# Mixer of a hybrid decoder step: loaded bias tables, HGRN2 factors on VectorE, row sums in two short-format passes, a fifth block-product pair

## The chip, the core and the metric

The kernel runs on one core of one Trainium2 chip. The metric is the device time of one execution in microseconds (us); the time given for a kernel is the median of its runs. The engines are named as in the profile: PE (TensorE, matrix products; PEld is its weight load), DVE (VectorE), ACT (ScalarE), POOL (GpSimd) and SP (SyncE, which here only issues DMAs). SBUF is the memory on the chip, in 128 partitions; PSUM, in eight banks, takes the matmul results, and POOL cannot read it.

## The reference, cut to what matters

One layer works on 544 tokens: 512 of a prompt and 8 x 4 of a sample group. The model width is 1024; the mixer has 8 attention heads of 64 and 4 HGRN2 heads of 128.

```
h = RMSNorm(x); z = h @ W_in        # 28 tiles of 128 columns: q, k, v (4 each), HGRN2 q, f, i, gate (4 each)
# dilated attention: three patterns (128,1), (512,4), (2048,16), penalty -m_h * distance, combined by
#   their softmax denominators; then every head RMS-normalised
# HGRN2: f = lb + (1-lb)*sigmoid(z_f); S_t = diag(f_t) S_{t-1} + (1-f_t) outer i_t;
#   o_t = S_t^T silu(q_t) / sqrt(128); per-head RMSNorm, times silu(gate)
x += [attn ; hgrn] @ W_out
x += CrossAttn(RMSNorm(x); 256 memory rows, K/V made from RMSNorm(mem)) @ W_co
x += W_down( silu(conv3(RMSNorm(x) W_gate)) * (RMSNorm(x) W_up) )
y = RMSNorm(x)
```

The three patterns are one softmax over all keys up to the query, with a bias: key distance d gets -m_h * d + ln(number of patterns that hold d). For the prompt this bias, for a block of 128 queries, is one table of 128 x 512 per head; the blocks use its right-hand parts.

## The kernel before, in words

Activations lie transposed (channels on partitions, 544 tokens along the free dimension). Most products are done in a short format: a matrix is split into a high part (a copy to float32r, on ACT) and a low part (the difference, on DVE), and a product is three passes, high x high, high x low and low x high. A plain tile of `z` is 8 x 3 products for tokens 0 to 255 and as many for 256 to 543 (`CUTS`, `passes`, `half`, `dense`). Other products, the row sums among them, are done in full float32; the profile shows such a matmul as two records.

**Block products.** `MixPair` makes two tiles of `z` together. It cuts the two weight tiles into four half-depth blocks and the tokens into two halves of 272, and computes the result from seven block products of 12 short-format matmuls in place of eight, at the price of sums of weight blocks (`S1` to `S4`), their own high and low parts, and sums of results. The token-side blocks are made once (`blocks_in`). `MIX_ORDER` lists the tiles in order; names that stand together are such a pair (four pairs in the kernel before), the others are plain tiles (`proj_in`). `ready` starts what can begin with a tile: `prompt_attention` for a v tile, `hgrn` when a head has its four tiles.

**Attention.** `prompt_attention(p, ...)` handles two heads. It makes their two bias tables on DVE, each with one `scalar_tensor_tensor` of the constants `dist` and `lnc`. Then, for three groups of query blocks: scores on PE, bias and row maximum on DVE, exp on ACT, normalisation on DVE, transposes and the value products on PE. Last it squares the output, sums it over each head's 64 rows by a matmul with a 0/1 matrix (`rsqrt_rows` with `blk64`) and scales.

**HGRN2.** `hgrn(h, ...)` works in seven levels of doubling width w (1 to 64; `level_ops`). At each level, DVE multiplies k by G and q by f, POOL multiplies half of G by the last f of the neighbouring half, and DVE multiplies half of f by the other's last. The f product writes what the POOL operation reads, so it waits for it. PE takes the products of the level (`level_products`). `hgrn_norm` ends a head with squares, a row sum (`rsqrt_rows` with `ones`, once per cut) and the gate.

**Norms.** `NextNorm` collects the squares of a new x, tile by tile, in `acc` (`SumSq`): ACT squares, POOL adds. `rows(c)` then takes the row sum of a cut with `rsqrt_rows`. The first norm of the kernel (`r_mix`), the memory's and the final one do their own full-format sums.

**Decode attention and order.** The sample group's attention over its cache (`decode_attention`) streams some 30 MB from memory as a side work of the mixer, in small products. What sets the order is `Tape`: it records all instructions as steps with dependencies and estimated lengths, and then plans one order per engine queue. PE's main steps (the tiles) keep their order; side steps on PE are put in as bursts, and the other queues take, among the steps that are ready, the one due first. `LEAD` is how far ahead of its due time a step may be taken, `MARGIN` the time to spare before a main step, `BURST` and `PATIENCE` say when a burst begins; `SLACK` gives steps their due time and is stored with each step as it is recorded. `run` plans `ROUNDS` = 4 orders, the due times of the second to fourth taken from the starts of the one before, and emits the one with the earliest planned end of PE. Tiles of kind "a" share `NA` = 59 buffers, weights 3 raw and 2 high and low ones, and PSUM banks fall into three kinds ("dense", "aux", "dec"). All compute instructions go through one wrapper line, L642, so the profile tells them apart by the names of their tiles.

Of the kernel before, what the change touches and what calls it, by code (L numbers as in the profile page):

```python
# [42 lines left out]
FW = 564  # L43
NA = 59

# [16 lines left out]
MIX_RAW = 3  # L62
MIX_ORDER = ('i0', 'q0', 'q1', 'q2 q3', 'k0 k1', 'k2 k3', 'f1 Q1', 'v0', 'g1', 'i1', 'v1', 'f2', 'Q2', 'g2', 'i2', 'v2', 'f3', 'Q3', 'g3', 'i3', 'v3')
WO_ORDER = (4, 5, 6, 0, 1, 7, 2, 3)
# [17 lines left out]
for _n, _c in (("ident", 128), ("ones", 128), ("blk64", 128), ("dist", 512), ("lnc", 512), ("dbias", NR + 2 * NS),  # L82
               ("mask_a", 96), ("mask_b", 96), ("mask_s", 96), ("batch", 4), ("h8", 8), ("h4", 4), ("sel8", 16),
               ("sel4", 16), ("sel32", 32), ("own", 2)):
    _span(CST_COLS, _n, _c)
# [10 lines left out]
def _log_counts(d):  # L96
    c = _counts(d)
    return np.where(c > 0, np.log(np.maximum(c, 1)), NEG)


def _constants():
# [11 lines left out]
    dist = 384 + p[:, None] - np.arange(512)[None, :]  # L113
    put("dist", dist.astype(np.float32))
    put("lnc", _log_counts(dist))
    slopes = 2.0 ** -(np.arange(NH) + 1.0)
    h = (p % 32) // TS
    t = p % TS
# [133 lines left out]
class Tape:  # L252
# [6 lines left out]

    ROUNDS = 4  # L260
    BURST, PATIENCE, SLACK, LEAD, MARGIN = 1.0, 4.0, 12.0, 15.0, 4.0
# [151 lines left out]
    def run(self):  # L413

        scale = sum(s.length for s in self.steps if s.engine == "PE") / sum(s.length for s in self.mains)
        t = 0.0
        for s in self.mains:
            s.est = t
            t += s.length * scale
        best = None  # L420
        for _ in range(self.ROUNDS):
            done = self.order()
            end = max(s.end for s in done if s.engine == "PE")
            if best is None or end < best[0]:
                best = end, done
            for s in self.mains:
                s.est = s.start
        for s in best[1]:
            for call in s.calls:
                call()  # L430
        self.live = False
        return done
# [214 lines left out]
def tile_decoder_step(ctx: ExitStack, tc: tile.TileContext, xT, memT, kwT, vw, s0, conv_in, mkT, mv, vecs, cst,  # L647
# [42 lines left out]
    nc.scalar.dma_start(vec, vecs)  # L690
    mid = CST_COLS["dist"][0]
    cs = tape.tile(one, [128, mid], F32, name="cs")
    cs2 = tape.tile(strm, [128, NCST - mid], F32, name="cs2")
    eps = tape.tile(one, [128, 1], F32, name="eps")
# [170 lines left out]
    def split_plain(src, name):  # L865
# [3 lines left out]
        return hi, lo  # L869

    def rsqrt_rows(acc, c0, c1, mat, width, r, name):

        for n0, m in ((c0, c1 - c0),) if c1 - c0 <= 512 else CUTS:
            ps = PX(f"psr_{name}_{n0}")
            nc.tensor.matmul(ps[:, :m], mat, acc[:, n0:n0 + m], start=True, stop=True)
            nc.scalar.activation(r[:, n0:n0 + m], ps[:, :m], AF.Ln, bias=eps, scale=1.0 / width)
            nc.scalar.activation(r[:, n0:n0 + m], r[:, n0:n0 + m], AF.Exp, scale=-0.5)
# [54 lines left out]
    with tape.as_written():  # L932
# [12 lines left out]
        for i in range(3):  # L945
            ws.load(i)
        nc.sync.dma_start(cs2, cst[:, mid:])
        for _ in range(AHEAD - 1):
# [34 lines left out]


    lbt = tape.tile(strm, [128, 4, 4], F32, name="lbt")
    l0 = vec[:, VEC_COLS["lb0"][0]:VEC_COLS["lb0"][1]]
# [271 lines left out]
    def decode_finish(out):  # L1258
# [18 lines left out]
        nc.scalar.activation(sq[:, :128], flat, AF.Square)  # L1277
        rsqrt_rows(sq, 0, 128, C("blk64"), 64, r, "attS")
        nc.vector.tensor_tensor(flat, flat, r[:, :128], op=ALU.mult)
# [9 lines left out]
    def prompt_attention(p, q, k, v):  # L1289
# [4 lines left out]
        for hh in range(2):  # L1294
            nc.vector.scalar_tensor_tensor(bias[hh][:, :512], C("dist"), -(2.0 ** -(2 * p + hh + 1)), C("lnc"),
                                           op0=ALU.mult, op1=ALU.add)
        S, P, T, PT, dens = {}, {}, {}, {}, {}
# [87 lines left out]
        nc.scalar.activation(sq[:, :SEQ], po, AF.Square)  # L1385
        rsqrt_rows(sq, 0, SEQ, C("blk64"), 64, r, f"att{p}")
        nc.vector.tensor_tensor(att[:, :SEQ], att[:, :SEQ], r[:, :SEQ], op=ALU.mult)
# [6 lines left out]
    def hgrn(h, f, q, gt, v):  # L1394
# [25 lines left out]
        def level_ops(w):  # L1420
# [12 lines left out]
            last = half(f, 1)[:, :, w - 1:w].to_broadcast([128, nb, w])  # L1433
            nc.gpsimd.tensor_tensor(half(G, 0), half(G, 0), last, op=ALU.mult)
            last = half(f, 0)[:, :, w - 1:w].to_broadcast([128, nb, w])
# [139 lines left out]
    def hgrn_norm(h, o, gt):  # L1575
# [3 lines left out]
        r = A(f"hr{h}")  # L1579
        for n0, n in CUTS:  # L1580
            rsqrt_rows(sq, n0, n0 + n, C("ones"), 128, r, f"hg{h}")
        nc.vector.tensor_tensor(o[:, :N], o[:, :N], r[:, :N], op=ALU.mult)
# [133 lines left out]
    class NextNorm:  # L1716


        def __init__(self, gain, name):
            self.gain, self.name, self.ssq, self.r = gain, name, SumSq(name, nc.gpsimd), A(f"r_{name}")  # L1720
            self.hl = [None] * KT
# [8 lines left out]
        def rows(self, c):  # L1730
            n0, n = CUTS[c]
            rsqrt_rows(self.ssq.acc, n0, n0 + n, C("ones"), D, self.r, self.name)

# [685 lines left out]
```

## Time and profile before

| what | value |
|---|---|
| median of 3 runs | 826.87 us (825.66 to 828.18) |
| profiled execution | 827.21 us, of which the span of instructions 825.4 us |
| mean granted TensorE clock | 0.996 |
| DMA | 132.32 MB, mean 160 GB/s |
| table loads on ACT | 11, 1283 ns each |

In the profile a group of instructions has its engine, operation, the names written and read (buffer numbers left out), shapes, count, busy time and mean; "idle before" is how long the engine sat without work ahead of such an instruction, with what ended that. Matmuls overlap, so the length of one record is longer than the step from one start to the next; the same holds, by some 0.07 us, for DVE. The mixer ends at about 316 us, where the `ps_wo` products begin; cross attention follows to 442, the first plain FFN tiles to 488, the FFN's block products and down products to 792, and the last down products and the final norm to the end.

### The profile page before, as it was taken

Reading aid. Unit: us, or ns where it says so; the run is one execution under the profiler, and the core shown is the slowest. Engines: PE = TensorE matmul, PEld = TensorE weight load, DVE = VectorE, ACT = ScalarE, POOL = GpSimd, SP = SyncE. Lnnn points to the kernel's source line nnn. Section 1 sums busy time; section 2 is a strip of 40 time slices with the busy share of each in tenths; the row PEclk is TensorE's granted clock in tenths of the full one; section 3 lists DMA queues with packets and bytes.
Section 4 is the critical chain, followed back from the end, with each engine's and each line's share of the span. In section 5 each row is a group of like instructions: output and inputs, shape, how many; then the busy total and the mean of one; then the engine's idle time right before and its main releaser. Section 6 shows DMA issues by size and latency. Waiting matters only on the chain.

```text
span 825.4 us, 18881 instructions
## 1 busy us (share of the span) xinstructions
PE 813.9 (99%) x7551; PEld 762.4 (92%) x7551; DVE 617.2 (75%) x1316; ACT 419.0 (51%) x835; POOL 148.0 (18%) x239
## 2 busy tenths in 40 slices
PE   9999999999999999999999999999999999999996
PEld 9999877887888889999889998999999999999995
DVE  6987889866879887564576998976777677767754
ACT  7643455434458345444545456554554455545533
POOL 0030211110210200222323131121112111211013
PEclk9999999999999999999999999999999999999999
DMA  9439999557823444260721347456456645653503
GB/s 343 156 121 297 352 287 304 166 170 226 289 81 110 158 145 153 59 218 31 256 86 53 103 103 203 130 131 176 118 140 181 139 116 145 163 149 83 164 1 109
DMA packets 90759, 132.32 MB, mean 160 GB/s; under 512 B 6064, under 2 KB 60080, under 8 KB 90544
## 3 DMA queue, kind: packets, MB, share of 16 engines
q1 hardware_dynamic: 84480, 120.69, 45.8%
q0 software_dynamic: 5184, 9.44, 7.2%
q8 instruction: 59, 0.97, 0.5%
q10 hardware_dynamic: 1008, 0.99, 0.4%
q14 instruction: 28, 0.23, 0.1%
HBM read 123.03 MB, written 8.07 MB: 159 GB/s over the span
## 4 chain that ended last, share of the span: by engine, by line
PE 91%; DVE 3%; ACT 2%; DMA 2%; issue 0%; SPq 0%; DVEq 0%; ACTq 0%
PE ps_d L642 13%; PE ps_au L642 6%; PE ps_ag L642 6%; PE ps_wo L642 6%; PE ps_cu L642 3%; PE ps_cg L642 3%; PE ps_z_v L642 3%; PE ps_co L642 3%; PE ps_g L642 3%; PE ps_cq L642 3%; PE ps_dz L642 3%; PE ps_u L642 3%; PE ps_z_g L642 2%; PE ps_z_i L642 2%; PE psdo L642 2%; PE psd L642 2%
## 5 line engine op out<-in xcount | busy, mean ns | idle before, releaser
L642 ACT CAST wh<-wr 128x1024 fp32r<-128x1024 f32 (+1 forms) x60 | 52.5, 889 | 73.6 <-issue 12.9
L642 DVE TENSOR_TENSOR wl<-wr,wh 128x1024 fp32r<-128x1024 f32 (+1 forms) x60 | 63.1, 1064 | 9.2 <-ACT wh L642 8.6
L642 DVE TENSOR_TENSOR xr<-xr,ps_d 128x256 f32<-128x256 f32 x80 | 34.5, 434 | 37.6 <-PE ps_d L642 37.5
L642 POOL COPY last<-ug 128x2 f32<-128x2 f32 (+1 forms) x44 | 14.7, 366 | 160.9 <-DVE ug L642 133.9
L642 DVE SCALAR_TENSOR_TENSOR cv<-ug,vec,cv 128x560 f32<-128x560 f32 x44 | 35.1, 798 | 8.1 <-ACT cv L642 7.8
L642 POOL TENSOR_TENSOR hG<-hG,z_f 128x256 f32<-128x256 f32 (+1 forms) x21 | 18.9, 899 | 118.9 <-DVE kq L642 63.5
L642 ACT ACTIVATE cv<-cv 128x560 f32<-128x560 f32 x22 | 14.8, 673 | 19.9 <-DVE cv L642 19.9
L642 ACT ACTIVATE cv<-ug,vec 128x560 f32<-128x560 f32 x22 | 18.8, 856 | 10.6 <-DVE ug L642 9.7
L617 POOL DMA_DIRECT2D S1u<-in_w_up x9 | 7.8, 862 | 89.4 <-DMA S1u<-in_w_up 45.3
L642 ACT ACTIVATE P<-P,mx 128x128 f32<-128x128 f32 (+3 forms) x32 | 17.7, 553 | 11.9 <-DVE mx L642 11.8
L642 POOL TENSOR_TENSOR acc_cx<-acc_cx,sq_cx 128x256 f32<-128x256 f32 (+1 forms) x14 | 11.4, 819 | 59.1 <-ACT sq_cx L642 59.0
L642 POOL COPY ug<-conv_state 128x16 f32<-128x16 f32 x22 | 18.4, 837 | 4.9 <-PE ps_u L642 2.8
L642 PE MATMUL ps_co<-coh,wh 128*128 128x256 f32 (+1 forms) x64 | 19.0, 297 | 0.0
L642 PE MATMUL ps_co<-coh,wl 128*128 128x256 f32 (+1 forms) x64 | 18.4, 288 | 0.0
L642 PE MATMUL ps_co<-col,wh 128*128 128x256 f32 (+1 forms) x64 | 18.4, 288 | 0.0
L642 POOL COPY qbd_win<-z_q 64x32 f32<-64x32 f32 x8 | 8.2, 1024 | 51.1 <-DVE z_q L642 50.9
L642 DVE TENSOR_TENSOR xr<-xr,ps_wo 128x256 f32<-128x256 f32 (+1 forms) x16 | 6.8, 435 | 13.9 <-PE ps_wo L642 13.8
L642 PE MATMUL psdo<-st,dpt 128*32 128x256 f32 x224 | 16.4, 386 | 0.0
L642 DVE TENSOR_TENSOR xr<-xr,ps_dz 128x288 f32<-128x288 f32 (+1 forms) x16 | 7.0, 436 | 12.3 <-PE ps_dz L642 12.3
L642 POOL TENSOR_TENSOR acc_ux<-acc_ux,sq_ux 128x256 f32<-128x256 f32 (+1 forms) x14 | 11.7, 834 | 20.9 <-ACT sq_ux L642 20.8
L642 PE MATMUL psd<-st,qbd_win 128*32 128x224 f32 x256 | 15.3, 358 | 0.0
L642 ACT ACT_TABLE_LOAD x11 | 14.1, 1283 | 2.3 <-issue 2.2
(3122 smaller groups left out, 3635.0 us busy)
## 6 DMA issues: line engine op xcount, KB each, us to landing
st<-in_kwT SPq DMA_DIRECT2D x32, 448.0 KB, 6.2
st<-in_vw SPq DMA_DIRECT2D x28, 512.0 KB, 5.7
wr<-in_w_in SPq DMA_DIRECT2D x17, 512.0 KB, 6.4
wd<-in_w_down SPq DMA_DIRECT2D x32, 256.0 KB, 2.8
wrg<-in_w_gate SPq DMA_DIRECT2D x9, 512.0 KB, 5.9
wru<-in_w_up SPq DMA_DIRECT2D x9, 512.0 KB, 4.6
st<-in_mkT SPq DMA_DIRECT2D x8, 512.0 KB, 6.8
wr<-in_w_out SPq DMA_DIRECT2D x8, 512.0 KB, 3.8
```

The costliest lines, as they stand in the source:

```text
L617: return tape.put(engine, lambda: call(*args, **kw), outs, ins, 0.1, 0.3, size)
L642: return tape.put(engine, lambda: call(*args, **kw), outs, ins, length, lag, size, port, words)
```

## The change

- **Bias tables.** The constants `dist` and `lnc` (512 columns each) are dropped, and eight finished tables (512 columns each) are laid behind the other constants in memory. `prompt_attention` loads its two with two DMAs of 256 KB on SP's queue instead of computing them. The early load of constants ends before these tables.
- **HGRN2 factors.** The product on G in `level_ops` goes from POOL to DVE.
- **Row sums.** `rsqrt_rows` splits the squares into a high part (a copy on ACT) and a low part (a subtraction on DVE), and sums both with a float32r copy of the 0/1 matrix, two short-format matmuls for one full-format one. The 0/1 matrices are copied once (`sum_operands`). `hgrn_norm` calls it once for all 544 columns; the matmuls inside are still cut in two.
- **Norm squares.** `NextNorm` lets DVE, and no longer POOL, add the squares. The final norm keeps POOL.
- **Fifth pair.** `v0` and `g1`, plain tiles before, become the pair `g1 v0`.
- **Order.** `run` plans 32 orders: the first with the constants as they are, the others with drawn values of `SLACK`, `LEAD`, `MARGIN`, `BURST` and `PATIENCE`. A draw that finds no order is left out. Due times are no longer taken from the order before. The random numbers have a fixed seed, so that the same order comes out each time.
- `NA` goes from 59 to 60 buffers.

```diff
-NA = 59
+NA = 60
-MIX_ORDER = (... 'f1 Q1', 'v0', 'g1', 'i1', 'v1', ...)
+MIX_ORDER = (... 'f1 Q1', 'g1 v0', 'i1', 'v1', ...)
...
-    put("dist", dist.astype(np.float32))
-    put("lnc", _log_counts(dist))
     slopes = 2.0 ** -(np.arange(NH) + 1.0)
+    put("bias", np.concatenate([(-s * dist + _log_counts(dist)).astype(np.float32) for s in slopes], 1))
...
-    ROUNDS = 4
+    DRAWS = 32
...
-        best = None
-        for _ in range(self.ROUNDS):
-            done = self.order()
+        best, draw = None, random.Random(0)
+        for i in range(self.DRAWS):
+            if i:
+                self.SLACK, self.LEAD, self.MARGIN = (draw.uniform(*r) for r in ((9.0, 16.0), (12.0, 19.0), (3.0, 6.0)))
+                self.BURST, self.PATIENCE = draw.uniform(0.6, 1.5), draw.uniform(2.5, 6.0)
+            try:
+                done = self.order()
+            except AssertionError:
+                continue
             end = max(s.end for s in done if s.engine == "PE")
             if best is None or end < best[0]:
                 best = end, done
-            for s in self.mains:
-                s.est = s.start
...
+    sums = {n: tape.tile(one, [128, 128], F32R, name=f"{n}_r") for n in ("ones", "blk64")}
+
+    def sum_operands():
+        for n, t in sums.items():
+            nc.scalar.copy(t, C(n))
+
     def rsqrt_rows(acc, c0, c1, mat, width, r, name):
+        hi, lo = R(f"sqh_{name}{c0}"), R(f"sql_{name}{c0}")
+        nc.scalar.copy(hi[:, c0:c1], acc[:, c0:c1])
+        nc.vector.tensor_tensor(lo[:, c0:c1], acc[:, c0:c1], hi[:, c0:c1].bitcast(F32), op=ALU.subtract)
         for n0, m in ((c0, c1 - c0),) if c1 - c0 <= 512 else CUTS:
             ps = PX(f"psr_{name}_{n0}")
-            nc.tensor.matmul(ps[:, :m], mat, acc[:, n0:n0 + m], start=True, stop=True)
+            for i, t in enumerate((hi, lo)):
+                nc.tensor.matmul(ps[:, :m], sums[mat], t[:, n0:n0 + m], start=i == 0, stop=i == 1)
...
-        nc.sync.dma_start(cs2, cst[:, mid:])
+        nc.sync.dma_start(cs2, cst[:, mid:end])
...
         for hh in range(2):
-            nc.vector.scalar_tensor_tensor(bias[hh][:, :512], C("dist"), -(2.0 ** -(2 * p + hh + 1)), C("lnc"),
-                                           op0=ALU.mult, op1=ALU.add)
+            nc.sync.dma_start(bias[hh][:, :512], cst[:, end + 512 * (2 * p + hh):end + 512 * (2 * p + hh) + 512])
...
-            nc.gpsimd.tensor_tensor(half(G, 0), half(G, 0), last, op=ALU.mult)
+            nc.vector.tensor_tensor(half(G, 0), half(G, 0), last, op=ALU.mult)
...
-        for n0, n in CUTS:
-            rsqrt_rows(sq, n0, n0 + n, C("ones"), 128, r, f"hg{h}")
+        rsqrt_rows(sq, 0, N, "ones", 128, r, f"hg{h}")
...
-            self.gain, self.name, self.ssq, self.r = gain, name, SumSq(name, nc.gpsimd), A(f"r_{name}")
+            self.gain, self.name, self.ssq, self.r = gain, name, SumSq(name), A(f"r_{name}")
```

More of the change, by code (lines that the diff above doesn't have):

```diff
@@ L1 @@
 import math
+import random
 from contextlib import ExitStack, contextmanager
@@ L62 @@
 MIX_RAW = 3
-MIX_ORDER = ('i0', 'q0', 'q1', 'q2 q3', 'k0 k1', 'k2 k3', 'f1 Q1', 'v0', 'g1', 'i1', 'v1', 'f2', 'Q2', 'g2', 'i2', 'v2', 'f3', 'Q3', 'g3', 'i3', 'v3')
+MIX_ORDER = ('i0', 'q0', 'q1', 'q2 q3', 'k0 k1', 'k2 k3', 'f1 Q1', 'g1 v0', 'i1', 'v1', 'f2', 'Q2', 'g2', 'i2', 'v2', 'f3', 'Q3', 'g3', 'i3', 'v3')
 WO_ORDER = (4, 5, 6, 0, 1, 7, 2, 3)
@@ L81 @@
     _span(VEC_COLS, _n, _c)
-for _n, _c in (("ident", 128), ("ones", 128), ("blk64", 128), ("dist", 512), ("lnc", 512), ("dbias", NR + 2 * NS),
+for _n, _c in (("ident", 128), ("ones", 128), ("blk64", 128), ("dbias", NR + 2 * NS),
                ("mask_a", 96), ("mask_b", 96), ("mask_s", 96), ("batch", 4), ("h8", 8), ("h4", 4), ("sel8", 16),
-               ("sel4", 16), ("sel32", 32), ("own", 2)):
+               ("sel4", 16), ("sel32", 32), ("own", 2), ("bias", 512 * NH)):
     _span(CST_COLS, _n, _c)
@@ L690, in tile_decoder_step @@
     nc.scalar.dma_start(vec, vecs)
-    mid = CST_COLS["dist"][0]
+    mid, end = CST_COLS["dbias"][0], CST_COLS["bias"][0]
     cs = tape.tile(one, [128, mid], F32, name="cs")
-    cs2 = tape.tile(strm, [128, NCST - mid], F32, name="cs2")
+    cs2 = tape.tile(strm, [128, end - mid], F32, name="cs2")
     eps = tape.tile(one, [128, 1], F32, name="eps")
@@ L982, in tile_decoder_step @@
             first_products(KT - 1)
+    sum_operands()
     lbt = tape.tile(strm, [128, 4, 4], F32, name="lbt")
@@ L1277, in decode_finish @@
         nc.scalar.activation(sq[:, :128], flat, AF.Square)
-        rsqrt_rows(sq, 0, 128, C("blk64"), 64, r, "attS")
+        rsqrt_rows(sq, 0, 128, "blk64", 64, r, "attS")
         nc.vector.tensor_tensor(flat, flat, r[:, :128], op=ALU.mult)
@@ L1385, in prompt_attention @@
         nc.scalar.activation(sq[:, :SEQ], po, AF.Square)
-        rsqrt_rows(sq, 0, SEQ, C("blk64"), 64, r, f"att{p}")
+        rsqrt_rows(sq, 0, SEQ, "blk64", 64, r, f"att{p}")
         nc.vector.tensor_tensor(att[:, :SEQ], att[:, :SEQ], r[:, :SEQ], op=ALU.mult)
@@ L1731, in rows @@
             n0, n = CUTS[c]
-            rsqrt_rows(self.ssq.acc, n0, n0 + n, C("ones"), D, self.r, self.name)
+            rsqrt_rows(self.ssq.acc, n0, n0 + n, "ones", D, self.r, self.name)
     cross_in = NextNorm("norm_cross", "cx")
```

## The prediction

> **What bounds the kernel now.** I read the page's head first, then the chain of waits, then the busy time by stage. From the page, the span, the busy shares and the chain's shares by engine:
>
> ```profile
> span 825.4 us, 18881 instructions
> PE 813.9 (99%) x7551; PEld 762.4 (92%) x7551; DVE 617.2 (75%) x1316; ACT 419.0 (51%) x835; POOL 148.0 (18%) x239
> PE 91%; DVE 3%; ACT 2%; DMA 2%; issue 0%; SPq 0%; DVEq 0%; ACTq 0%
> ```
>
> The matmul engine is busy nearly all the time and carries nine tenths of the chain. By stage (columns: stretch and length in us, busy time of PE, weight load, DVE, ACT, POOL, then granted clock, DMA share, GB/s); the last row is the whole mixer after its first products:
>
> ```profile
> 97.00:145.00 48.00, 48.00 (x710) 37.09 (x703) 43.20 (x143) 23.70 (x58) 9.24 (x11) 1.00 0.93 301
> 250.00:290.00 40.00, 40.00 (x498) 35.48 (x496) 36.64 (x101) 24.63 (x49) 6.60 (x7) 1.00 0.47 142
> 306.20:309.60 3.40, 3.40 (x10) 2.68 (x10) 1.88 (x4) 1.89 (x5) 0.00 (x0) 0.50 0.65 216
> 316.00:442.00 126.00, 126.00 (x1024) 119.32 (x1023) 75.19 (x145) 58.99 (x147) 32.73 (x41) 1.00 0.41 133
> 488.00:792.00 304.00, 302.50 (x2404) 301.70 (x2403) 232.26 (x432) 159.65 (x297) 48.22 (x106) 1.00 0.55 142
> 20.00:316.00 296.00, 294.36 (x3431) 251.69 (x3430) 245.61 (x618) 149.62 (x305) 43.57 (x52) 0.99 0.63 201
> ```
>
> The reader is to see three things. PE has no gaps to give back, so a gain must come from products taken away. DVE is second: 90% in 97 to 145 and 92% in 250 to 290, with 296.0 - 245.6 = 50.4 us idle over the mixer. And one short stretch, 306.2 to 309.6, ran at half the clock with PE busy throughout. The few real stalls show in the chain and in PE's timeline (start, length, what; the chain's rows come first):
>
> ```profile
> 90.69 1.28 ACT L642
> 92.43 1.77 PE ps_af1Q L642 x12
> 91.35 0.24 PE L642 MATMUL psd<-knew,qbd_win 128*32 128x32 f32 x8
> 502.68 0.39 PE L642 MATMUL ps_d<-h3h,wd_0h 128*128 128x256 f32 x1
> 503.45 0.38 PE L642 MATMUL ps_d<-h3l,wd_0h 128*128 128x256 f32 x1 [0.38 <-DVE h3l L642]
> 505.16 0.29 PE L642 MATMUL ps_du<-B21h,wlu 128*128 128x272 f32 x1
> 506.35 0.39 PE L642 MATMUL ps_au<-Uh,S2u4h 128*128 128x272 f32 x1 [0.91 <-ACT S2u4h L642]
> ```
>
> A table load on ACT, ahead of a copy that PE needs, holds PE from about 91.5 to 92.43, 0.9 us. At 502.68 and 505.16 the next product comes after 0.77 and 1.19 in place of 0.12: 1.7. Half of the half-speed window is 1.7. Together 4.3 us.
>
> **Row sums on PE.** One such sum stands alone among 256-column products (timeline of PE; start, length, names, x records):
>
> ```profile
> 367.26 0.28 PE L642 MATMUL ps_cq<-cx7h,wl 128*128 128x256 f32 x1
> 367.38 0.59 PE L642 MATMUL psr_cx<-acc_cx,cs 128*128 128x256 f32 x2
> 367.62 0.48 PE L642 MATMUL ps_cq<-cx0h,wh 128*128 128x256 f32 x1
> 367.93 0.28 PE L642 MATMUL ps_cq<-cx0l,wh 128*128 128x256 f32 x1
> 368.05 0.28 PE L642 MATMUL ps_cq<-cx0h,wl 128*128 128x256 f32 x1
> ```
>
> From 367.26 to 367.93 lie 0.67 us; two ordinary products at 0.12 each (367.93 to 368.05) are 0.24, so the full-format sum costs 0.43 for 256 columns. Two short-format passes cost what two ordinary products do, 0.24: 0.19 saved, 0.74 ns a column. The columns are 4 x 512 (attention), 128 (its sample part), 4 x 544 (HGRN) and 2 x 544 (the two norms): 5,440, so **-4.0 us**. Bounds: nothing, if a wait fills the place (below), and -4.5, if the 128 + 544 columns that ran in the half-speed stretch save twice (rows of the chain):
>
> ```profile
> 307.34 0.43 PE psr_attS L642 x2
> 307.76 1.81 PE psr_hg L642 x4
> ```
>
> **The fifth pair on PE.** Rows of the chain: a plain tile of 48 products in the mixer, one in the FFN, a block product of 12:
>
> ```profile
> 163.59 6.22 PE ps_z_f L642 x48
> 467.10 6.02 PE ps_g L642 x48
> 84.17 1.51 PE ps_cf1Q L642 x12
> ```
>
> Two tiles are 12.0 to 12.4; seven block products 7 x 1.51 = 10.6. That is -1.5 to -1.9; I take **-1.7**, since in the mixer the tiles are broken by bursts as z_f is.
>
> **What DVE, ACT and POOL get.** Groups by form, the POOL factors by tile (durations min/median/max), and the timeline of DVE and POOL where a factor runs:
>
> ```profile
> L642 POOL TENSOR_TENSOR hG<-hG,z_f x21: 620/779/1576, 124.9 to 288.7; 128x256 f32<-128x256 f32 x15, 128x272 f32<-128x272 f32 x6
> L642 POOL TENSOR_TENSOR hG<-hG,hf x7: 651/721/1242, 96.8 to 137.3; 128x256 f32<-128x256 f32 x5, 128x272 f32<-128x272 f32 x2
> L642 POOL TENSOR_TENSOR acc_cx<-acc_cx,sq_cx 128x256 f32<-128x256 f32 x7 | 5.4, 770 | 40.8 <-ACT sq_cx L642 40.7
> L642 DVE SCALAR_TENSOR_TENSOR bias<-cs 128x512 f32<-128x512 f32 x8 | 6.0, 745 | 0.0
> L642 ACT CAST wh<-wr 128x512 fp32r<-128x512 f32 x22 | 13.0, 617 | 11.9 <-PE ps_cs L642 5.3 <-PE ps_cp L642 2.7 <-DMA wr<-in_w_out 1.6
> 115.64 0.41 DVE L642 TENSOR_TENSOR kq<-hk,hG 128x256 f32<-128x256 f32 x1
> 115.97 0.41 DVE L642 TENSOR_TENSOR kq<-hq,hf 128x256 f32<-128x256 f32 x1
> 116.31 1.16 DVE L642 SCALAR_TENSOR_TENSOR bias<-cs 128x512 f32<-128x512 f32 x1
> 118.95 0.68 DVE L642 SCALAR_TENSOR_TENSOR bias<-cs 128x512 f32<-128x512 f32 x1
> 119.55 0.45 DVE L642 TENSOR_TENSOR z_g<-ps_z_g,r_mix 128x288 f32<-128x288 f32 x1
> 116.20 0.72 POOL L642 TENSOR_TENSOR hG<-hG,hf 128x256 f32<-128x256 f32 x1 [10.08 <-DVE kq L642]
> ```
>
> On DVE an operation of 256 elements takes a step of 0.34 (115.64 to 115.97 to 116.31), one of 512 a step of 0.60 (118.95 to 119.55); by the line through both, 1024 take 1.1 and 544 take 0.63. The 28 factors move over: +28 x 0.35 = +9.8. The bias tables leave: -8 x 0.60 = -4.8. Low parts of the row sums: 4 x 0.60 + 4 x 0.63 + 0.2 = +5.1. The pair has five half-size low parts and four sums for one whole low part (9 x 0.60 - 1.1 = +4.3), and seven evacuations for four (+1.0). The mixer's DVE gets +15.4 against 50.4 idle. ACT gets eight row-sum copies at about 0.62 and the pair's five casts and three copies for one whole cast, some 8 us against 296.0 - 149.6 idle. POOL loses 28 x 0.75 = 21 us that no one waits for long. In the norms DVE takes 28 adds at 0.35 and four low parts, +11, against 126.0 - 75.2 = 50.8 idle; each add is 0.4 shorter than POOL's 0.77, which pays about a third of the copy, subtraction and hand-over (some 1.3 us) now ahead of each sum. In the trace the first norm sum's products began at 367.38, and the two 256-column tiles around it had no use for its result until both banks were full: this cover hides it. Without it, 1.3 us for each of four sums.
>
> The wait that is removed is DVE's on the factor: one level's chain loses POOL's 0.75 and a hand-over and gains 0.35, seven times a head, about 3 us. What is late next there is the level's own products, which DVE feeds. I cost it at nothing, because PE has plain tiles to run meanwhile.
>
> A factor on POOL also slows DVE: the bias operation beside POOL's factor took 1.16 where the other took 0.68. The Trainium skill says so in "SBUF — State Buffer", "SBUF: two separate sides": a DVE instruction with two SBUF inputs and a GpSimd instruction that reads SBUF lock each other out for a whole instruction. By that rule the move gives back up to 28 x 0.48 = 13 us of DVE time, so that the mixer's DVE would get 2 us and not 15; PE's sum would be the same.
>
> **Bias loads on SP.** DMA issues by size and median us to landing:
>
> ```profile
> hst<-in_s SPq DMA_DIRECT2D x8, 256.0 KB, 7.1
> wd<-in_w_down SPq DMA_DIRECT2D x32, 256.0 KB, 2.8
> ```
>
> Eight loads of 256 KB stand in SP's queue among the weights and the cache; 0.5 MB of constants leave the early load. Net 1.6 MB at 301 GB/s is 5 us of a DMA that has 0.93 busy until 145 and 0.54 or so after; the cache stream slides by that and catches up. The new wait is the softmax's first DVE operation on its table. Behind it in DVE's queue stand evacuations, for which PE's next tile waits. A load takes 2.8 to 7.1 us; it has no input, so it can go out before its tile's products, which alone take 6. I cost it at 0, bounds 0 and +4 (one late load, 7.1 - 2.8, for the two heads in the busy stretch together).
>
> **The order.** Every queue gets a new order. The first of the 32 draws uses the old constants and the old clock, so it is the first of the four rounds of before; the other three rounds, which retimed the clock, are gone. The drawn SLACK changes nothing, because each step keeps the value it was recorded with; the others do. The order can win or lose stalls, 4.3 us in all: bounds -4.3 (all gone) and +4.3 (as many new ones); I take **-0.5**.
>
> **The sum**: -4.0 - 1.7 - 0.5 = -6.2. The profiled execution took 827.2 (825.4 span and 1.8 around it), 0.3 above the median of the runs, 826.9: 821.0 for it, **820.7** for the median.
>
> **Rivals.** (1) *DVE takes over in the mixer*, and the kernel is slower. The place is the two stretches at 90 and 92%, where the idle is 4.8 and 3.4 us and the pair, one or two heads' factors and low parts all land. If all of the added 15.4 comes out on PE, 836; from 6.2/15.4 = 0.4 on nothing is gained, and at 0.6 it is 820.7 + 9.2 = 830. For it: the shares. Against it: 42 us idle elsewhere, and the lock-out above that goes. (2) *Late operands*: row sums that now pass ACT and DVE first, and bias loads. Half of the eight mixer sums holding PE by 1.3 us each are +5: 826. For it: in-order queues; against: PE always had plain tiles ready. (3) *The half-speed window goes* (the order moves the small products of 301 to 305 apart): with the other old stalls shortened, 817. (4) *More such windows*: two more, 820.7 + 3.4 = 824. Thinner PE work speaks for it, the fact that only one came in 300 us of mixer against. The Trainium skill, "TensorE: Matmul & The Clock Gate", Part 1, has the clock halve after an idle window of 3.4 us; here the window's length agrees, 3.4, but PE was not idle before it, so the trace goes further than the rule. (5) *The draws change nothing*: without the -0.5, 821.2.
>
> **Chances.** Forecast with (4) and (5), 818 to 824.4: 0.52. (3), below 818: 0.17. (2), within 0.3% (2.5 us, about what can be told from no change): 0.15. (1), above 829.4: 0.16. So faster 0.69, same 0.15, slower 0.16. The range 815.5 to 828.5 leaves out the best and most of (1); the likeliest's own range is 818 to 824.4.
>
> **What would show it.** Row sums as two records of about 0.28 from a high and a low part, with an insertion of 0.24 per 256 columns; two ps_z tiles fewer and seven products of g1 and v0; no factor on POOL and 28 more operations of 0.41 on DVE; DVE's mixer sum near 261. Wrong would be: PE gaps named by DVE in 97 to 145 or 250 to 290 (1), by psr's operands or a bias DMA (2), or the same matmul counts as before.

## The result, and the profile after

The changed kernel takes 825.13 us (median of 20 runs, 822.2 to 827.6) where the kernel before, run beside it, takes 827.41 (20 runs, 825.49 to 830.16). The ratio is 0.9973 [0.9962, 0.9984]: 2.3 us less, 0.27%. The interval leaves out 1, so it is faster, but by little more than a third of the 6.2 us forecast, and by less than the 0.3% that the prediction called a difference. The profiled execution took 825.25 us with a span of 823.5.

The head of the page of the changed kernel, and its chain of waits by engine:

```profile
span 823.5 us, 18847 instructions
PE 808.6 (98%) x7539; PEld 760.7 (92%) x7539; DVE 627.8 (76%) x1388; ACT 428.6 (52%) x857; POOL 103.8 (13%) x183
PE 88%; DVE 4%; DMA 4%; ACT 3%; issue 0%; POOL 0%; ACTq 0%; DVEq 0%; SPq 0%; POOLq 0%
```

PE's work fell by 813.9 - 808.6 = 5.3 us, the two product terms (5.7) but for 0.4; each of the two profiles holds one half-speed window, so these cancel. The span fell by only 1.9. The chain says the same: PE's part fell from 91% to 88%, and DVE, ACT and DMA together rose from 7% to 11%. The 3.4 us between 5.3 and 1.9 are new idle time of PE (span less busy time: 11.5 before, 14.9 after). By stage (columns as in the prediction: stretch, length, busy time of PE, weight load, DVE, ACT, POOL, then clock, DMA share, GB/s):

```profile
97.00:140.00 43.00, 42.20 (x658) 35.86 (x656) 38.21 (x123) 23.56 (x47) 3.13 (x5) 1.00 0.90 302
245.00:285.00 40.00, 40.00 (x428) 35.18 (x427) 38.61 (x108) 25.94 (x54) 0.00 (x0) 1.00 0.48 143
20.00:311.50 291.50, 288.37 (x3424) 249.57 (x3424) 253.40 (x660) 156.60 (x324) 19.23 (x25) 1.00 0.66 212
311.50:438.40 126.90, 125.55 (x1022) 118.52 (x1021) 78.88 (x173) 60.66 (x150) 11.34 (x15) 1.00 0.42 132
484.00:789.00 305.00, 303.44 (x2403) 303.00 (x2402) 231.69 (x433) 160.71 (x298) 52.05 (x106) 0.99 0.54 141
504.00:507.40 3.40, 3.40 (x17) 3.40 (x16) 3.36 (x6) 2.66 (x6) 0.00 (x0) 0.50 0.33 57
```

The mixer ends 4.5 us earlier (311.94 in place of 316.47, the first `ps_wo` product). Of this, 1.7 is the half-speed window, which no longer stands there; the other 2.8 stand against 4.9 of product terms in the mixer (5.7 less 0.8 for the two norms) and 1.6 of new idle time there. From 245 to 285 DVE is busy 97% and PE still 40.00 of 40.00. The rows below are the later stages: cross attention has 1.35 us of PE idle where before it had none, and among the FFN's first block products a half-speed window has appeared. First products by stage, before and after, each from that stage's tile (between `ps_cq` and `ps_co` the lead falls by more than the idle time, since side work has moved there; by `ps_ag` this has come back):

| stage | before | after | lead |
|---|---|---|---|
| `ps_wo`, out of the mixer | 316.47 | 311.94 | 4.5 |
| `ps_cq`, cross attention | 364.55 | 359.93 | 4.6 |
| `ps_co` | 405.89 | 403.40 | 2.5 |
| `ps_ag`, first FFN pair | 487.81 | 484.25 | 3.6 |
| `ps_dz`, last down products | 791.55 | 789.18 | 2.4 |

**The cross-attention norm.** The timeline of all engines from the end of `ps_wo` on (start, length, engine, names; in brackets the idle time before it and what ended it):

```profile
360.12 0.46 DVE L646 TENSOR_TENSOR xr<-xr,ps_wo 128x288 f32<-128x288 f32 x1 [1.62 <-PE ps_wo L646]
360.50 0.69 DVE L646 TENSOR_TENSOR wl<-wr,wh 128x512 fp32r<-128x512 f32 x1
361.10 0.79 DVE L646 TENSOR_TENSOR acc_cx<-acc_cx,sq_cx 128x256 f32<-128x256 f32 x2
361.61 0.41 ACT L646 CAST sqh_cx<-acc_cx 128x256 fp32r<-128x256 f32 x1
362.60 0.42 DVE L646 TENSOR_TENSOR sql_cx<-acc_cx,sqh_cx 128x256 fp32r<-128x256 f32 x1
362.75 0.28 PE L646 MATMUL ps_cq<-cx0h,wh 128*128 128x256 f32 x1
365.46 0.28 PE L646 MATMUL ps_cq<-cx7h,wl 128*128 128x256 f32 x1
365.57 0.28 PE L646 MATMUL psr_cx<-sqh_cx,ones_r 128*128 128x256 f32 x1
365.69 0.28 PE L646 MATMUL psr_cx<-sql_cx,ones_r 128*128 128x256 f32 x1
365.81 0.30 PE L646 MATMUL psr_cx<-sqh_cx,ones_r 128*128 128x288 f32 x1
365.94 0.29 PE L646 MATMUL psr_cx<-sql_cx,ones_r 128*128 128x288 f32 x1
366.07 0.47 ACT L646 ACTIVATE r_cx<-psr_cx,eps 128x256 f32<-128x256 f32 x1 [2.85 <-PE psr_cx L646]
367.50 0.70 PE L646 MATMUL ps_cp<-mk,cq 128*128 128x256 f32 x2 [1.27 <-DVE cq L646]
```

The squares of the first cut's tokens are there at 358.64, and DVE sits idle until 360.12, but in its queue the adds stand behind the last evacuation and a weight's low part. The low part of the squares is there at 363.02. The gap between the two `ps_cq` tiles, where the old sum stood, was at 362.75: missed by 0.3 us. The sum then waits out a whole tile, until 365.57: PE takes its queue in the planned order, and the plan has put the sum behind the second tile. The root, the scaling and `cq` come behind it, and PE stands from 365.94 + 0.13 to 367.50: 1.43 us from start to start, of which the row counts 1.27 as idle.

**The first block products of the FFN.** The chain of waits there (start, length, what):

```profile
492.92 7.23 DMA S3u<-in_w_up
500.17 0.62 ACT S3u4h L646
500.79 0.55 ACT Vh L646
501.34 0.52 ACT S1u4h L646
501.86 0.53 ACT S2u4h L646
```

And PE's own timeline at the gap:

```profile
500.79 0.29 PE L646 MATMUL ps_du<-B21h,wlu 128*128 128x272 f32 x1
502.43 0.39 PE L646 MATMUL ps_au<-Uh,S2u4h 128*128 128x272 f32 x1 [1.35 <-ACT S2u4h L646]
```

The second sum of weight blocks, a DMA of 7.23 us, lands at 500.15, and four casts on ACT end with the one that PE needs: 1.64 us between products in place of 0.13, a stall of 1.5. As much was lost at this place before (PE idle 1.50 from 500 to 508; now 1.56). What is new is the half-speed window behind it, 504.0 to 507.4. The smaller losses show in other stretches of the chain: ahead of the first pair, and at the table load of the first HGRN2 head:

```profile
44.80 0.69 DVE S2q2q L646
45.49 0.62 DVE S3lq2q L646
46.11 0.35 DVE z_q L646
46.59 1.74 PE ps_aq2q L646 x12
...
104.92 1.28 ACT L646
106.22 1.17 ACT ds L646 x2
107.43 1.09 PE psdt L646 x8
```

In idle time of PE, as the rows of its timeline count it: DVE's sums hold it for 0.65 ahead of 46.59, where before there was no wait. Ahead of 107.43 the table load holds it for 0.80, as it did ahead of 92.43 before (0.84). A decode product waits 0.53 for its cache transfer (201.39), which is new, and a wait for `z_q` has grown by 0.33 (0.78 ahead of 41.59 before, 1.11 ahead of 42.48 now). With the cross norm's 1.27, these are 2.8 of the 3.4 us. Of the rest, 0.45 lies behind PE's last product (6.96 us from its end to the end of the span before, 7.42 now), and the other 0.2 is in waits of 0.1 and less.

### The profile page after: what moved, and what is told of

It is laid out like the page before. It is cut to its first block, busy times and chain, and to the rows that moved or that the text cites. A ratio compares the mean times of both kernels' runs of the same rounds, so it can differ in the third digit from the quotient of the medians.

```text
span 823.5 us, 18847 instructions
## 1 busy us (share of the span) xinstructions
PE 808.6 (98%) x7539; PEld 760.7 (92%) x7539; DVE 627.8 (76%) x1388; ACT 428.6 (52%) x857; POOL 103.8 (13%) x183
## 4 chain that ended last, share of the span: by engine, by line
PE 88%; DVE 4%; DMA 4%; ACT 3%; issue 0%; POOL 0%; ACTq 0%; DVEq 0%; SPq 0%; POOLq 0%
PE ps_d L646 13%; PE ps_au L646 6%; PE ps_ag L646 6%; PE ps_wo L646 6%; PE ps_cu L646 3%; PE ps_cg L646 3%; PE ps_g L646 3%; PE ps_dz L646 3%; PE ps_u L646 3%; PE ps_co L646 3%; PE ps_z_v L646 2%; PE ps_z_i L646 2%; PE ps_cq L646 2%; PE ps_z_Q L646 2%; PE psdo L646 2%; PE ps_z_f L646 1%
## 5 line engine op out<-in xcount | busy, mean ns | idle before, releaser
L646 ACT CAST wh<-wr 128x1024 fp32r<-128x1024 f32 (+1 forms) x58 | 50.5, 886 | 61.4 <-issue 11.5
L646 DVE TENSOR_TENSOR wl<-wr,wh 128x1024 fp32r<-128x1024 f32 (+1 forms) x58 | 58.4, 1017 | 8.7 <-ACT wh L646 8.3
L646 POOL TENSOR_TENSOR hvm<-hsm,cs 64x512 f32<-64x512 f32 x4 | 5.7, 1431 | 167.0 <-ACT hsm L646 167.0
L646 POOL COPY ug<-conv_state 128x16 f32<-128x16 f32 x22 | 21.0, 954 | 23.7 <-PE ps_co L646 19.3
L646 POOL TENSOR_SCALAR cp<-cp,cden 128x256 f32<-128x256 f32 x8 | 7.9, 988 | 89.1 <-DVE cden L646 89.1
L646 DVE CUSTOM_DVE_ANT_0 P<-psS,bias 128x128 f32<-128x128 f32 (+3 forms) x32 | 14.4, 484 | 0.4 <-PE psS L646 0.2
```

The lines of the kernel that those rows point to most:

```text
L646: return tape.put(engine, lambda: call(*args, **kw), outs, ins, length, lag, size, port, words)
```

## The experiments

The theory after the result: the product terms came off, and the order (with the place it gives the cross norm's sum) took the rest. The rivals: DVE's added work, the loaded tables, the fifth pair's late operands. All kernels compute the whole reference. Times are medians; each ratio is to the kernel before, run on the same chip between them, with its 95% interval.

**The same kernel again, and its first order alone.** The second plans only one order, with the constants as they are.

```diff
-    DRAWS = 32
+    DRAWS = 1
```

> The changed kernel once more, nothing edited. Theory A (the products came off as worked out, and some 3 us of them went back in new waits of PE): the ratio to before is 0.997 again, PE busy near 808.6 us, and of the waits seen in the first trace those set by the order of the queues come back at the same products: 1.4 us at the first cross scores behind the norm's row sum, 1.0 us at the table load of head 0 during the fifth pair, 0.8 us ahead of the first pair. The wait at the first FFN pair's sums and the half-speed window, which hang on DMA landings and on the phase of the clock, may move. Rival B (the lost 4 us are noise of single executions): the waits lie elsewhere, and the ratio moves toward 0.9925.

> The changed kernel with one planned order in place of 32: the constants as they are. If the choice among the draws is worth what I took (0.5 us), 825.6 us, 0.9979 of before. Rival C (the drawn order is what costs: it fits the planner's lengths and not the chip's): this one is faster, 821 to 822, and lacks the 1.4 us wait at the first cross scores. Rival D (the draws carry the whole gain): 827.4.

Again: 825.37, 0.9968 [0.9955, 0.9981]. The waits at the cross scores (1.27 us idle), at the table load (0.80) and ahead of the first pair (0.66) come back at the same products, and so does the stall at the first FFN pair (1.53, ahead of 501.71); the half-speed window doesn't. First order: 822.78, 0.9934 [0.9916, 0.9951]. The same instructions in the first order are some 2.6 us faster than in the order that was chosen as the best of 32. The first order keeps the cross norm's wait (1.27 idle) and most of the table load's (0.64), but has none ahead of the first pair and only 0.4 at the first FFN pair.

**The draws in the kernel before, and other draws in the changed one.** One takes the new planning loop over into the kernel before; the second draws with another seed; two more emit one given order of the 32: draw 4, which the planner puts last, and draw 14, which it puts level with the chosen one.

```diff
-    ROUNDS = 4
+    DRAWS = 32          # and the loop of the change
...
-        best, draw = None, random.Random(0)
+        best, draw = None, random.Random(1)
...
+            if i != 4:
+                continue
...
+            if i != 14:
+                continue
```

> The kernel before with the new choice among 32 orders and none of the other edits. Theory A: PE's products are the old ones (busy 813.9), so 826 to 828, ratio 0.998 to 1.001. Rival C: slower than before, over 1.002. Rival D: 825, 0.997.

> The changed kernel with another seed for the 32 draws, so that another order of the same instructions is taken. Theory A says that which waits arise is a matter of the order: PE busy 808 to 809 again, other waits, and a time within 2 us of 825.1 on either side. If the waits come with the operations themselves (a longer chain ahead of each row sum, more work on DVE), the same waits return at the cross scores and the time is the same within 0.5 us.

> The changed kernel in the order of draw 4 of the 32, the one planned to end last. If the planned end ranks orders: slower than the chosen order's 825.1, ratio above 0.9973, up to 1.003. Theory C (it does not): anything between 0.992 and 0.998, as the first order and the other seed gave.

> The changed kernel in the order of draw 14, planned to end as early as the chosen one within a fraction of a tenth of a per cent. If the planned end ranks orders: 0.997, as the chosen one. Theory C: it may differ from the chosen one by 2 us or more, most likely to the fast side (0.993 to 0.995), and its waits lie at other products.

Draws in the kernel before: 827.15, 0.9993 [0.9982, 1.0004], no change. Other seed: 823.51, 0.9943 [0.9922, 0.9964]. Draw 4: 825.33, 0.9972 [0.9954, 0.9990]. Draw 14: 821.90, 0.9940 [0.9925, 0.9954]. Five orders of the same instructions thus lie at 0.9934, 0.9940, 0.9943, 0.9970 (the chosen one, mean of its two measurements) and 0.9972: mean 0.9952, standard deviation 0.0018, or 4.0 us gained on average with 1.5 us of scatter, in which the noise of the measurements (intervals of 0.0011 to 0.0021 to either side) has a part. The idle time of PE in the profiles, span less busy time, goes with it:

| order | ratio | PE idle, us |
|---|---|---|
| first order | 0.9934 | 12.7 |
| draw 14 | 0.9940 | 12.7 |
| other seed | 0.9943 | 12.5 |
| chosen order, two profiles | 0.9973, 0.9968 | 14.9, 14.4 |
| draw 4 | 0.9972 | 15.6 |

All five have the cross norm's wait, 1.27 us each time, with the four passes of the sum together behind the second `ps_cq` tile. In draw 4 the FFN norm's sum waits too: 0.70 for its low part at 429.67. The order that the planner ranked last ran like the one it ranked first, and the one it put level with that was faster. So its choice is worth nothing that can be seen in these orders, and here it fell on the slow side by 1.5 us.

**The row sums back in full format**, on the first order.

```diff
-            for i, t in enumerate((hi, lo)):
-                nc.tensor.matmul(ps[:, :m], sums[mat], t[:, n0:n0 + m], start=i == 0, stop=i == 1)
+            nc.tensor.matmul(ps[:, :m], C(mat), acc[:, n0:n0 + m], start=True, stop=True)
```

> As the base, but all row sums are full-format products of the squares again, with no high and low parts. Theory A: PE gets the 4.0 us back; the wait of 1.4 us at the first cross scores, which I put down to the longer chain ahead of the norm's row sum, goes, and the time is 822.8 + 4.0 - 1.4 = 825.4, ratio 0.9975. If that wait has another cause: 826.8, 0.9992, with the wait still there. Rival (the added copies and subtractions cost as much as the passes save): 823.

825.41, 0.9974 [0.9965, 0.9983], 3.3 us slower than the first order by the ratios and 2.6 by the medians, where 2.6 were forecast. PE is busy 813.0 where the first order has 808.4, and 1.7 of the latter is a half-speed window (clock 0.50 from 300.2 to 303.6) that this profile lacks, so the work is 6.3 us more. That is above the term of 4.0, but PE's busy time for the same instructions differs by 2.4 among the five orders (806.7 to 809.1, windows taken off), so the size of the term is better read where a sum stands alone (below). The cross norm's wait is absent here: both sums, with no links to pass, come between the two `ps_cq` tiles, at 366.23.

**The fifth pair back to two plain tiles**, on the first order.

```diff
-MIX_ORDER = (... 'f1 Q1', 'g1 v0', 'i1', ...)
+MIX_ORDER = (... 'f1 Q1', 'v0', 'g1', 'i1', ...)
```

> The changed kernel with the first planned order alone (the run before this one, 822.8 us, is its base), and v0 and g1 as plain tiles again. Theory A (PE's products set the time, part by part): the tiles' 12 products more cost 1.7 us, 824.5, ratio 0.9965. Rival (the pair's sums and splits on DVE and ACT eat its gain): 822 to 823, 0.993 to 0.995.

825.19, 0.9972 [0.9961, 0.9982]: the pair gains 2.4 us by the medians and 3.1 by the ratios, where 1.7 were forecast. PE's work rose by 1.0 (809.4 against 808.4, one half-speed window in each), and its idle time by 1.7, of which 1.15 is a wait ahead of 163.69 that is this order's own. Sign and size fit the forecast within the scatter of orders; no more can be said. DVE's mixer sum is 251.34 here and 254.25 with the pair.

**The G factors back on POOL.** The first order doesn't exist for this kernel (the planner finds none), so it is planned with all draws.

```diff
-            nc.vector.tensor_tensor(half(G, 0), half(G, 0), last, op=ALU.mult)
+            nc.gpsimd.tensor_tensor(half(G, 0), half(G, 0), last, op=ALU.mult)
```

> The changed kernel with the HGRN2 factors on POOL again (the first order does not exist for this program, so that an order of a later draw is taken). PE's products are unchanged. Theory A: 822.8 within 1.5 us, whichever order. If VectorE's load bounds the mixer, DVE loses 28 operations and the first cross tile begins earlier than at 361.1 us; if the chain through POOL holds PE at the end of the mixer, it begins 2 us or more later. The lock-out seen once in the trace before (an operation of 0.68 took 1.16 beside a factor on POOL) would show as a DVE sum that falls by less than 28 x 0.35 = 9.8 us.

821.47, 0.9930 [0.9916, 0.9943]. The mixer up to its last tile, with the factors on DVE (the first order; columns as above), and then the row of 21 of its factors in the view by tile (least, median and greatest length in ns):

```profile
20.00:313.10 293.10, 290.32 (x3429) 250.80 (x3427) 254.25 (x660) 156.09 (x324) 20.12 (x25) 0.99 0.64 211
```
```profile
L646 DVE TENSOR_TENSOR hG<-hG,z_f x21: 404/417/445, 143.7 to 284.4; 128x256 f32<-128x256 f32 x15, 128x272 f32<-128x272 f32 x6
```

The same two with the factors on POOL:

```profile
20.00:309.80 289.80, 288.06 (x3427) 250.15 (x3426) 250.92 (x631) 155.33 (x321) 45.57 (x53) 1.00 0.65 212
```
```profile
L646 POOL TENSOR_TENSOR hG<-hG,z_f x21: 622/777/1824, 141.0 to 281.5; 128x256 f32<-128x256 f32 x15, 128x272 f32<-128x272 f32 x6
```

28 operations have left DVE. Their records of 0.42 overlap, so that a step of 0.35 each counts, 9.8 us in all; but DVE's busy time is only 3.3 lower. The other 6.5 come back as longer operations beside POOL's: in this trace the 76 DVE operations that overlap a tensor operation of POOL take 8.7 us more than the median of their shape, and in the other there are 11, which take 2.0 more. This is the rule that the prediction quoted from the Trainium skill, "SBUF — State Buffer", "SBUF: two separate sides"; the trace agrees, with half of the 13 us that the prediction gave as its most. In time the move gains nothing that can be seen: this kernel, without it, is as fast as the fastest of the five orders with it. It keeps the cross norm's wait (1.26).

**A fixed place for the cross norm's row sum.** The sum of the first cut becomes one of PE's main steps, right behind the first `ps_cq` tile; on the first order, and then with all draws.

```diff
-    cross_in.rows(0)
-    cross_in.rows(1)
...
+        if h == 0 and n0 == 0:
+            with tape.main():
+                cross_in.rows(0)
+            cross_in.rows(1)
```

> As the base, but the row sum of the cross norm's first 256 tokens has a fixed place on PE, behind the first cq tile, and that of the other 288 follows as a side step. Theory A: the wait of 1.4 us ahead of the first cross scores comes from the sum having missed the gap between the first two cq tiles by a fraction of a microsecond and waiting a whole tile of 2.8 us; with the fixed place it shrinks to 0.3 or less: 821.5, ratio 0.992. If the wait comes from something else on the way (the scores' other operands), it stays and the time is 822.8.

> The kernel with the fixed place for the first cross row sum (819.5 us with the first order alone, 0.9909), now with the best of 32 orders as in the changed kernel. Theory C (the order with the earliest planned end is no better on the chip, and often worse): at 819.5 or above, up to 822. If the choice is worth its planned gain: below 819, ratio under 0.990.

First order: 819.49, 0.9909 [0.9893, 0.9925]. All draws: 820.26, 0.9910 [0.9895, 0.9925]. These two are the fastest kernels of the study. PE's timeline of the first:

```profile
364.36 0.28 PE L646 MATMUL ps_cq<-cx7h,wl 128*128 128x256 f32 x1
364.48 0.28 PE L646 MATMUL psr_cx<-sqh_cx,ones_r 128*128 128x256 f32 x1
364.60 0.28 PE L646 MATMUL psr_cx<-sql_cx,ones_r 128*128 128x256 f32 x1
364.71 0.28 PE L646 MATMUL ps_cq<-cx0h,wh 128*128 128x256 f32 x1
367.55 0.29 PE L646 MATMUL psr_cx<-sqh_cx,ones_r 128*128 128x288 f32 x1
367.68 0.30 PE L646 MATMUL psr_cx<-sql_cx,ones_r 128*128 128x288 f32 x1
367.82 1.46 PE L646 MATMUL ps_cp<-mk,cq 128*128 128x256 f32 x6
```

The first sum stands between the two tiles, and `ps_cp` follows at once. Its two passes put in 0.23 us (364.48 to 364.71), where the full-format sum put in 0.43: the saving that was forecast. 32 draws are again no better than the one order.

**The norms' adds back on POOL**, which takes the other link out of the same chain; on the first order.

```diff
-            self.gain, self.name, self.ssq, self.r = gain, name, SumSq(name), A(f"r_{name}")
+            self.gain, self.name, self.ssq, self.r = gain, name, SumSq(name, nc.gpsimd), A(f"r_{name}")
```

> As the base, but POOL adds the squares of the two norms again. Theory A: each add is some 0.4 us longer, so the cross norm's row sum is ready later still, but it already waits for the end of the second cq tile: the same 1.4 us wait, 822.8 within 1. If the adds on DVE, which stand behind other work in its queue, are what made the sum late, the wait goes and the time is 821.4.

820.89, 0.9921 [0.9906, 0.9936]. Its timeline at the same place:

```profile
358.31 0.40 ACT L646 ACTIVATE sq_cx<-xr 128x256 f32<-128x256 f32 x1
358.85 0.74 POOL L646 TENSOR_TENSOR acc_cx<-acc_cx,sq_cx 128x256 f32<-128x256 f32 x1 [5.05 <-ACT sq_cx L646]
360.95 0.59 DVE L646 TENSOR_TENSOR sql_cx<-acc_cx,sqh_cx 128x256 fp32r<-128x256 f32 x1
363.24 0.28 PE L646 MATMUL psr_cx<-sqh_cx,ones_r 128*128 128x256 f32 x1
366.45 0.29 PE L646 MATMUL psr_cx<-sql_cx,ones_r 128*128 128x288 f32 x1
366.58 0.59 PE L646 MATMUL ps_cp<-mk,cq 128*128 128x256 f32 x2
```

POOL's add takes 0.74, where DVE's takes 0.4, but begins 0.14 behind its square, since nothing stands ahead of it. The low part is there at 361.54, the sum makes the gap at 363.24, and the wait is gone, against theory A.

**Both edits, and the fixed place with the factors on POOL.** The edits are those above, on the first order.

> The first order alone, the fixed place for the first cross row sum, and the norms' adds on POOL again. Theory A: both cures remove the same wait of 1.4 us, so together they give no more than one: 819.5 to 821, ratio 0.990 to 0.9925. If the earlier adds also help at the FFN's norm: 818, 0.989.

> The fixed place for the first cross row sum, the first order alone, and the HGRN2 factors on POOL. In the last runs DVE's busy time over the mixer was the same with the factors on either engine (254.1 us), so by theory A this is 819.5 within 1, ratio 0.990 to 0.992. If POOL's side is the better one, as 821.5 against 822.8 suggests: 818, 0.989. If the move to DVE pays where the cross wait does not hide it: 821 or more.

Both: 822.24, 0.9941 [0.9923, 0.9959]. Fixed place and factors on POOL: 823.67, 0.9953 [0.9938, 0.9968]. Neither has the cross wait, and neither is faster than one cure alone. (The 254.1 us of the last expectation is read up to 313, past the end of that mixer; up to its own end DVE's sum is 250.92.) Each of these edits gives every queue another order. Two orders with a scatter of 1.5 us differ by 2.1 (standard deviation); by the ratios the first kernel is 1.7 and 2.6 us slower than its two parts alone, the second 1.9 and 3.6. The last is much even for that; its trace has new waits of PE in the mixer, 0.71 ahead of 269.80 and 0.70 ahead of 297.60. So the cures remove the wait in all five traces, while in time no pair of kernels shows it cleanly. The five kernels without the wait have a mean ratio of 0.9927, the five orders with it 0.9952: 2.1 us, with a standard error of about 1. That fits a wait of 1.4, and would fit twice as much.

**The tables computed on DVE again.** The two constants take room, so it runs with 58 buffers, and 58 buffers alone are run beside it.

```diff
-            nc.sync.dma_start(bias[hh][:, :512], cst[:, end + 512 * (2 * p + hh):end + 512 * (2 * p + hh) + 512])
+            nc.vector.scalar_tensor_tensor(bias[hh][:, :512], C("dist"), -(2.0 ** -(2 * p + hh + 1)), C("lnc"),
+                                           op0=ALU.mult, op1=ALU.add)
...
-NA = 60
+NA = 58
```

> The changed kernel with its first order alone (base: 822.8 us, 0.9934), and the bias tables computed on DVE from the two constants again instead of loaded; the constants take room, so 58 shared buffers in place of 60. PE's products are those of the base. Theory A: DVE has room for 8 x 0.60 = 4.8 us, so 822.8 within 1. If the loads held the softmax up: 1 to 4 us faster. If DVE's load counts: up to 4.8 slower.

> The changed kernel with its first order alone and 58 shared buffers in place of 60, nothing else (base: 822.8 us, 0.9934). If the two buffers were what made the kernel with computed tables slow: 825 to 826, 0.997 to 0.998. If the computing did it: 822.8 within 1, 0.993 to 0.995.

Tables on DVE: 826.04, 0.9981 [0.9969, 0.9994], slower than theory A had it. 58 buffers alone: 824.40, 0.9964 [0.9950, 0.9977], between the two cases of the expectation. By the ratios, 2.5 of the 3.9 us that the first lost to the kernel with 60 buffers came with the buffers and their new order alone. The intervals overlap. Whether the loaded tables gain anything by themselves stays open; that they cost nothing fits the trace of the changed kernel, where the softmax never waits for one (its DVE operations on a table wait 0.2 us in all, for scores).

## Why the prediction was right or wrong

**Row sums, -4.0: right.** A pass takes a step of 0.12 for 256 columns (365.57, 365.69, 365.81), two of them put in 0.23 in place of 0.43, and taking the edit back costs PE more than the 4.0 (6.3, uncertain by some 2). **Fifth pair, -1.7: right** as far as it can be told (1.0 in PE's work). With both, PE has 5.3 us less to do, against 5.7.

**"This cover hides it": wrong, and this is the first step that failed.** The prediction costed the norms' new links (add on DVE, copy, low part) at nothing, because the tile behind the sum had no use for its result. It looked at the time from the sum to its use and not at when the sum could start. The 1.3 us of links were near (1.5 from the add's end to the low part's). But the add now stands in DVE's order behind the last evacuation and a weight's low part, the sum misses the gap between two tiles, and its place in PE's queue is the next gap, 2.8 us later. A delay of 0.3 us became a wait of 1.4. The traces show it: the wait is gone with the sum in a fixed place, with the adds on POOL and with full-format sums, and it is there in every kernel of the study that has the short passes and neither cure (1.3 to 1.5 us idle). It is rival (2) in mechanism, in one of the four norm sums of the changed kernel, and in none of the eight of the mixer that it priced.

**The order, -0.5: wrong, the second step that failed.** With -2.3 measured, -5.7 of products and +1.4 of the cross wait, +2.0 is left for it: inside the bounds of 4.3, on the wrong side. The chosen order is 1.5 slower than the mean of five and some 2.6 slower than the first. None of the old stalls went (the table load's is 0.80 for 0.84, the first FFN pair's 1.56 for 1.50), and three came or grew, by 0.65 + 0.53 + 0.33 = 1.5 of the 2.0. The prediction had no row for the sign of this term. What it took for granted, that the best of 32 draws is at least not worse than the first, does not hold: the planner's rank did not order the four draws that were run, and in the kernel before 32 draws changed nothing.

**The sum again**, with what the runs showed: -5.7 of products, +1.4 of the cross norm's wait, and +0.3 left over, for other waits in the mean of orders, make the measured mean of -4.0; the drawn order adds 1.5, which gives -2.5 (measured: -2.3, and -2.6 when run again). The five kernels with short passes and without the cross wait lie at a mean ratio of 0.9927, 6.0 us faster, where 6.2 were forecast; with orders that scatter by 1.5 us, so close a fit is in part luck.

**DVE, +15.4 in the mixer: mis-sized.** It measured 253.40 against 245.61, so +7.8; the low parts, the pair and the factors came, and some 6.5 us of lock-out went (15.4 - 6.5 = 8.9). The prediction's 261 left that gain out, and the 2 that it gave with the whole of it was too low. **Rival (1) falls**: DVE at 97% from 245 to 285 and PE without a gap. **Bias loads, 0: right**; they land in 4.6 to 8.5 us, and no PE wait stands behind them. **Rivals (3) and (4)**: the window left its place and came back at another, so their number stayed one. The move of the factors gains no time of its own that can be seen, as costed.

**Open**: what each order gains or loses is read from its trace as idle time of PE, but why one set of constants gives a better one isn't. Edits worth under some 2 us can't be told from the new order that they bring.

## What to carry to other kernels

When a plan puts side products only between PE's tiles, a late operand costs the rest of a tile, so for each sum compare the time its operands are ready with the next gap, through every queue that its links join, before calling it hidden. When an edit makes a planner give all queues a new order, measure several orders of the same instructions first; here they differ by 1.5 us (standard deviation), about as much as a single edit is worth. And a planner's "best of 32" is no gain until the first and the last of its ranks have been run as well.

## What the runs showed of the hardware

Half-speed windows came again. In the changed kernel one began 1.6 us after a stall of 1.5 (502.43 to 504.0); in its 3.4 us products of 288 columns follow each other by 0.24 us (504.92, 505.16), in place of 0.13. In the second execution of the same program the stall at this place was as long (1.53 idle), and no window came. In the kernel with the fixed place two lie end to end:

```profile
297.20:304.00 6.80, 6.80 (x22) 5.64 (x22) 3.43 (x11) 1.61 (x6) 0.00 (x0) 0.50 0.56 166
```

PE is busy 6.80 of 6.80 us at a clock of 0.50, and the window begins among small products (15 of 16 columns from 296.29 on). Each window of 3.4 us at half the clock costs 1.7. The second execution of the same changed program had none; PE was busy 1.6 us less (807.0 against 808.6), and its span was 821.4 us, 2.1 shorter. So one program has such a window in one execution and not in another, and one profiled execution doesn't tell its time to better than 2 us. The clock also halves when PE's work ends: in the kernel with the factors on POOL the last product ends at 811.6, and from 812.8 the clock is 0.50, after 1.2 us of idle. The rule of the Trainium skill, "TensorE: Matmul & The Clock Gate", Part 1, has the slower clock come after an idle window of some 3.4 us. Ahead of the window at 504 PE idled 1.56 of 3.4 us in two stalls, and in the 3.4 us ahead of the one in the kernel with the fixed place it was busy throughout, so the measurement stands against the rule, and what starts a window stays open.
